# Selecting the first pair's slots ahead of its product and the other slots behind it

## The chip, the cores and the metric

The kernel runs on one core of one Trainium2 chip. The metric is the device time in microseconds (us) of one execution; it is run several times and the median counts.

A core has five engines that follow their own instruction lists and wait for each other by semaphores: TensorE (PE, matrix products, with a separate stream of weight loads), VectorE (DVE), ScalarE (ACT), GpSimd (POOL) and SyncE (SP), whose list here is mostly transfers. Sixteen DMA engines carry the transfers.

## The reference

Two layers run one after the other: the first mixes tokens by a short convolution, the second by sparse attention, and each is followed by a hierarchical mixture of experts (MoE) and a layer norm. All 1024 tokens have 1024 features. The MoE is what matters here:

```python
g_top = jnp.argmax(g_logits, axis=-1)                 # one of 8 groups for each token
e_val, e_loc = lax.top_k(e_logits, TOPK_IN_GROUP)     # two of the 8 experts in it
gate = jax.nn.softmax(e_val, axis=-1) * g_gate
...
def expert_block(args):
    xb, e = args
    h = jax.nn.silu(xb @ w1[e]) * (xb @ w3[e])        # w1, w3: 1024 x 256
    return h @ w2[e]                                  # w2: 256 x 1024
...
out = jnp.zeros_like(xt).at[row_tok].add(ys * row_w[:, None].astype(ys.dtype))
```

There are 64 experts in each layer, and every one is computed. Inputs and outputs are 32 bit floats.

## The kernel before

The memory on the chip is cut into 26 equal slots of one megabyte (128 partitions x 2048 floats). `take` hands out the slot that has been free longest, `give` returns one; what is written into a slot waits for the last readers of what was there. The order of the instructions on each engine is the order in which the program is written.

`moe(l, ...)` (L794) computes one MoE. An expert has 64 places for tokens, two experts make a pair (32 pairs, `NP`), four pairs make a group (8 groups, `GP` = 4), so a group has 512 places. `gather` (L823) brings the rows of a group's 128 tokens from memory on POOL's queue; block `NG`, gathered second, holds tokens of any group that are over 128. `parts` (L832) makes 0/1 matrices `sel` on DVE and splits the gathered rows into a high and a low part, in two halves for the first group: ACT writes the high part (L210), DVE the low (L211).

`select` (L849) turns them into `gt`, the tokens of the group's 512 places, feature by place: for each of 8 tiles `k` of 128 features four products (two blocks x high and low) of 128 x 512 add up in one PSUM buffer `rg` (three of them), and DVE or ACT by turns copies it to `gt[k]`. For the first group `select` runs before all pairs, and for every other group in the last pair of the group ahead of it, between `turn` and `down`.

A pair is: `up` (L863), the product of its 128 places with w1 and w3 into `ph`; `act` (L877), Silu on ACT and a multiplication on DVE; `turn` (L881), two transposes on PE; `down` (L888), the product with w2, scaled by ACT and DVE into the slot `yslot` and, for an overflow, `bslot`; `add` (L915) adds the pair before to the sums of the group.

The weights are 192 matrices of one megabyte per MoE. `prefetch(l, keep)` (L783) starts loads, in the order in which the pairs need them, as long as more than `keep` slots are free; they go to SP's queue if no other is named. `up` and `down` give their slots back after each half. The stage starts with two gathers, then `prefetch(l, 3, eng=nc.gpsimd)`, `parts(0)`, four products that only warm PE (L89), `select()`, and `yslot, bslot = self.take(), self.take()`.

Of the kernel before, what the change touches and what calls it, by code (L numbers as in the profile page):

```python
# [23 lines left out]
F32 = mybir.dt.float32  # L24
# [4 lines left out]
AF = mybir.ActivationFunctionType  # L29
# [4 lines left out]
P = 128  # L34
T = 1024
D = 1024
# [30 lines left out]
class Net:  # L67
# [726 lines left out]
    def moe(self, l, out, last=None, split=None):  # L794
# [3 lines left out]
        nc, S, W = self.nc, self.slots, self.W  # L798
        R_ = lambda v: v.bitcast(F32R)
        mm = nc.tensor.matmul  # L800
        ctx = ExitStack()
        psh = ctx.enter_context(self.tc.tile_pool(name="ps_h", bufs=1, space=PSUM))
        psr = ctx.enter_context(self.tc.tile_pool(name="ps_r", bufs=3, space=PSUM))
        psc = ctx.enter_context(self.tc.tile_pool(name="ps_c", bufs=1, space=PSUM))
        xr = {}
        gts = [self.take() for _ in range(2)]
        ms, hs = self.take(), self.take()
        sel = [S[ms][:, b * 512:(b + 1) * 512] for b in range(2)]
        hg, hT, io = (S[hs][:, a:b] for a, b in ((1024, 1280), (1280, 1536), (1536, 2048)))
        pick = [S[ms][:, 1024 + i * 256:1024 + (i + 1) * 256] for i in range(4)]  # L810
        gt = [S[gts[k // 4]][:, (k % 4) * 512:(k % 4 + 1) * 512] for k in range(KT)]
        nc.gpsimd.iota(io, pattern=[[1, 512]], base=0, channel_multiplier=0,
                       allow_small_or_imprecise_dtypes=True)
        xs, sums, scat, kept = {}, {}, [], []
# [8 lines left out]
        def gather(b):  # L823

            if b == 1:
                xr[0] = self.take()
            idx = (self.rows0 if b in (0, 1, 2, NG) else self.rows)[:, b:b + 1]
            nc.gpsimd.indirect_dma_start(
                out=xrow(b), out_offset=None, in_=self.xn[:, :],
                in_offset=bass.IndirectOffsetOnAxis(ap=idx, axis=0), bounds_check=T - 1, oob_is_err=False)  # L830

        def parts(g):  # L832


            for i in range(2):
                o, c = sel[i], g + i * NG
                nc.vector.tensor_scalar(R_(o), io, self.codes[:, 0, c:c + 1], None, op0=OP.is_equal)
                nc.vector.scalar_tensor_tensor(R_(o), io, self.codes[:, 1, c:c + 1], o, op0=OP.is_equal, op1=OP.add)
            v = []
            for i, b in ((0, g), (1, NG))[:1 if g else 2]:  # L840
                s = xs[i] = self.take()
                v.append([xrow(b).rearrange("s (q k) -> s k q", k=KT),
                          *(S[s][:, j * D:(j + 1) * D].rearrange("s (k q) -> s k q", k=KT) for j in range(2))])
            w = KT if g else KT // 2
            for k in range(0, KT, w):
                for a in v:
                    self.split(*(b[:, k:k + w] for b in a))

        def select():  # L849

            for k in range(KT):
                pt = psr.tile([P, 512], F32, name="rg")
                for i in range(2):
                    for j in range(2):
                        mm(pt, R_(S[xs[i]][:, j * D + k * P:j * D + (k + 1) * P]), R_(sel[i]),  # L855
                           start=i == 0 and j == 0, stop=i == 1 and j == 1)
                if k % 2:
                    nc.scalar.activation(gt[k], pt, AF.Copy)
                else:
                    nc.vector.tensor_copy(gt[k], pt)  # L860
            self.give(xs[0])

        def up(p):  # L863
            o = p % GP * P
            ph = psh.tile([P, 512], F32, name="ph")
            for m in range(2):
                for k in range(KT):
                    for q in range(2):
                        w = S[W[2 * p + q, m]]
                        mm(ph[q * CAP:(q + 1) * CAP, m * 256:(m + 1) * 256],  # L870
                           gt[k][:, o + q * CAP:o + (q + 1) * CAP], w[:, k * 256:(k + 1) * 256],
                           start=k == 0 and m == 0, stop=k == KT - 1, skip_group_check=True)
                self.give(*[W.pop((2 * p + q, m)) for q in range(2)])
                self.prefetch(l, 1 if p < 3 else 0)
            return ph

        def act(p, ph):  # L877
            nc.scalar.activation(hg, ph[:, :256], AF.Silu)  # L878
            nc.vector.tensor_mul(hg, hg, ph[:, 256:])  # L879

        def turn(p):  # L881
            px = psr.tile([P, 512], F32, name="rg")
            hv = hg.rearrange("s (q c) -> s c q", c=2)
            for c in range(2):
                nc.tensor.transpose(px[:, c * P:(c + 1) * P], hv[:, c], self.ident)
            nc.scalar.activation(hT, px[:, :256], AF.Copy)  # L886
# [20 lines left out]
        def places(p):  # L907

            o = pick[p % GP]
            nc.vector.tensor_scalar(R_(o[:, :P]), io[:, :P], self.srank[:, p:p + 1], None, op0=OP.is_equal)  # L910
            if p >= NP - GP:
                nc.vector.tensor_scalar(R_(o[:, P:]), io[:, P:2 * P], self.sr7[:, p % GP:p % GP + 1], None,
                                        op0=OP.is_equal)

        def add(p, h):  # L915

            i = p % GP
            for b in range(2 if p >= NP - GP else 1):
                if i == 0:
                    sums[b, h] = psc.tile([P, 512], F32, name=f"pc{b}{h}")  # L920
                for j in range(2):
                    mm(sums[b, h], R_(pick[i][:, b * P:(b + 1) * P]),
                       R_(S[yslot][:, j * D + h * 512:j * D + (h + 1) * 512]),
                       start=i == 0 and j == 0, stop=i == GP - 1 and j == 1 and b == 0)
# [4 lines left out]
        def beyond(p):  # L929

            nc.gpsimd.indirect_dma_start(  # L931
                out=self.Yov[l][:, :], out_offset=bass.IndirectOffsetOnAxis(ap=self.ovi[:, p:p + 1], axis=0),
                in_=share(p), in_offset=None, bounds_check=2 * P - 1, oob_is_err=False)

        def load_beyond():
            for j in range(2):
                nc.sync.dma_start(S[bslot][:, j * D:(j + 1) * D], self.Yov[l][j * P:(j + 1) * P])

        def residual(b, h):
            v = xrow(b)[:, h * 512:(h + 1) * 512]  # L940
            nc.vector.scalar_tensor_tensor(v, v, ALPHA, sums[0, h], op0=OP.mult, op1=OP.add)
# [12 lines left out]
        def finish(b):  # L954

            st = ln_st()
            for h in range(2):
                self.ln_stats(xrow(b), st, h)
            self.ln_done(xrow(b), st)
            scatter(b)  # L960
# [4 lines left out]
        def scale_rows():  # L965
            kept.append(NG)
            a = [S[xs[1]][:, j * D:(j + 1) * D].rearrange("s (k q) -> s k q", k=KT) for j in range(2)]
            nc.vector.tensor_add(xrow(NG).rearrange("s (q k) -> s k q", k=KT), *a)
            nc.vector.tensor_scalar(xrow(NG - 1), xrow(NG - 1), ALPHA, None, op0=OP.mult)
# [6 lines left out]
        def residual_sums(k, stop=False):  # L976
            b, i = ends[k]
            for h in range(2):
                mm(sums[i, h], self.ident, xrow(b)[:, h * 512:(h + 1) * 512], start=False, stop=stop)
# [15 lines left out]

        for b in (0, NG):
            gather(b)
        self.prefetch(l, 3, eng=nc.gpsimd)
        parts(0)
        self.warm(psr, "rg", io, WARM[1])  # L1000
        select()
        yslot, bslot = self.take(), self.take()
        self.prefetch(l, 0)
        for p in range(NP):
            g, i = divmod(p, GP)
            if p == NP - 1:
                residual_sums(0)
            ph = up(p)
            act(p, ph)
            places(p)  # L1010
            if p:
                add(p - 1, 0)
            turn(p)
            if p:
                add(p - 1, 1)
            if p == NP - 2:
                scale_rows()
            if i == GP - 1 and g + 1 < NG:
                select()
            down(p)  # L1020
            if g < NG - 1:
                beyond(p)
            if g and i == 0:
                for h in range(2):
                    residual(g - 1, h)
                finish(g - 1)
            if p < 2:
                gather(p + 1)
            if 0 < g < NG - 2 and i == 2:
                gather(g + 2)  # L1030
            if p == 2:
                self.load_ln(self.i["ln2_g"][l], self.i["ln2_b"][l], nc.scalar)
            if p == GP + 2:
                self.count_over()
            if i == GP - 2 and g + 1 < NG:
                parts(g + 1)
            if last and p == NP - 1:
                last()
            self.prefetch(l, 0)
            if p == NP - 2:  # L1040
                load_beyond()
# [958 lines left out]
```

## Time and profile before

| | before |
|---|---|
| median of 3 runs | 2250.32 us (2249.17 to 2250.35) |
| the profiled execution | 2252.98 us |
| its span in the profile | 2251.2 us |
| PE busy | 2116.3 us, 94% |
| DVE, ACT, POOL busy | 52%, 38%, 18% |
| first MoE, second MoE (selecting products to last sums) | 414 to 905 us, 1750 to 2238 us |

Every time in the profile is counted from the start of the span. Busy time of PE contains products that overlap with the next one, so a run of products is best read by the starts of its first and last. "PEclk" is the clock that the throttle granted to PE, 1.00 for 2.4 GHz and 0.50 for 1.2 GHz. A wait names what ended last.

### The profile page before, as it was taken

How to read it: one execution, taken by the hardware profiler on the slowest of the kernel's cores; microseconds unless marked ns; L12 is line 12 of the kernel's file. 1: busy time of each engine (PE TensorE's matmuls, PEld its weight loads, DVE VectorE, ACT ScalarE, POOL GpSimd, SP SyncE). 2: the span in 40 equal slices, each digit the busy share in tenths (PEclk: the TensorE clock that was granted, in tenths of full speed). 3: DMA queues.
4: the chain of work that ended last, by engine and by line, in shares of the span. 5: the costliest groups of instructions: out<-in, count | busy, mean ns of one | idle time of the engine just before them, and what ended most of it. 6: DMA issues, size and time to landing. Idle time of an engine off the chain costs nothing. (4 is left out here: it accounts for less than half of the span.)

```text
span 2251.2 us, 32795 instructions
## 1 busy us (share of the span) xinstructions
PE 2116.3 (94%) x12541; PEld 1547.7 (69%) x12541; DVE 1164.0 (52%) x2760; ACT 846.3 (38%) x1714; POOL 394.9 (18%) x477
## 2 busy tenths in 40 slices
PE   8999999799999999699998999999997998999997
PEld 7888888455555555677886899998886555555553
DVE  4333478432333333567878877774488233333333
ACT  3111211232333331356895877763211332333321
POOL 0000011110111110522332544322012111111101
PEclk9999999899999999899998999999999999999998
DMA  5113275599999999212211000003335799999995
GB/s 160 50 55 114 98 271 189 214 419 420 418 419 419 420 418 397 101 38 66 56 29 75 1 1 20 1 19 118 118 128 205 291 418 420 419 418 419 420 419 247
DMA packets 136777, 502.63 MB, mean 223 GB/s; under 512 B 23339, under 2 KB 69651, under 8 KB 86948
## 3 DMA queue, kind: packets, MB, share of 16 engines
q1 hardware_dynamic: 116608, 461.86, 52.1%
q0 software_dynamic: 16128, 32.09, 3.8%
q10 hardware_dynamic: 3876, 6.51, 0.8%
q8 instruction: 100, 1.64, 0.3%
q14 instruction: 65, 0.53, 0.1%
HBM read 476.70 MB, written 51.40 MB: 235 GB/s over the span
## 5 line engine op out<-in xcount | busy, mean ns | idle before, releaser
L870 PE MATMUL ph<-slot,slot 128*64 128x256 f32 x4096 | 461.5, 382 | 13.0 <-DVE nx L771 8.6
L870 PEld LDWEIGHTS ph<-slot,slot 128*64 128x64 f32 x4096 | 297.5, 138 | 193.1 <-issue 48.9
L901 DVE SCALAR_TENSOR_TENSOR slot<-rg,sgate,slot 128x512 fp32r<-128x512 f32 x128 | 96.1, 751 | 300.7 <-ACT slot L900 299.7
L896 PE MATMUL rg<-slot,slot 128*64 128x512 f32 x1024 | 233.8, 598 | 4.1 <-ACT slot L886 1.3
L210 ACT ACTIVATE slot<-slot 128x1024 fp32r<-128x1024 f32 (+2 forms) x151 | 119.0, 839 | 246.8 <-DVE slot L372 148.1
L222 PE MATMUL ps<-slot,slot 128*128 128x512 f32 x512 | 203.0, 396 | 0.8 <-DVE slot L211 0.8
L224 PE MATMUL ps<-slot,slot 128*128 128x512 f32 x512 | 199.6, 390 | 0.0
L223 PE MATMUL ps<-slot,slot 128*128 128x512 f32 x512 | 199.6, 390 | 0.0
L222 PE MATMUL po<-slot,slot 128*128 128x256 f32 (+1 forms) x544 | 189.9, 349 | 0.4 <-DVE slot L1699 0.4
L931 POOL DMA_INDIRECT Yov<-slot,ovi x56 | 55.5, 991 | 727.5 <-ACT slot L903 727.5
L223 PE MATMUL po<-slot,slot 128*128 128x256 f32 (+1 forms) x544 | 181.5, 334 | 0.0
L224 PE MATMUL po<-slot,slot 128*128 128x256 f32 (+1 forms) x544 | 181.5, 334 | 0.0
L211 DVE TENSOR_TENSOR slot<-slot,slot 128x1024 fp32r<-128x1024 f32 (+2 forms) x146 | 125.3, 895 | 89.9 <-ACT slot L210 88.8
L896 PEld LDWEIGHTS rg<-slot,slot 128*64 128x64 f32 x1024 | 67.8, 136 | 139.5 <-issue 114.6
L879 DVE TENSOR_TENSOR slot<-slot,ph 128x256 f32<-128x256 f32 x64 | 26.9, 420 | 232.9 <-ACT slot L878 232.9
L222 PE MATMUL pa<-slot,slot 128*128 128x512 f32 (+1 forms) x384 | 144.4, 376 | 0.2 <-DVE slot L211 0.2
L224 PE MATMUL pa<-slot,slot 128*128 128x512 f32 (+1 forms) x384 | 143.2, 373 | 0.0
L223 PE MATMUL pa<-slot,slot 128*128 128x512 f32 (+1 forms) x384 | 143.2, 373 | 0.0
L900 ACT ACTIVATE slot<-rg,sgate 128x512 fp32r<-128x512 f32 x128 | 87.6, 684 | 133.5 <-PE rg L896 133.5
L211 DVE TENSOR_TENSOR slot<-pT,slot 128x512 fp32r<-128x512 f32 (+1 forms) x160 | 101.6, 635 | 70.0 <-ACT slot L210 68.7
L855 PE MATMUL rg<-slot,slot 128*128 128x512 f32 x512 | 126.0, 403 | 6.2 <-ACT slot L210 4.1
L878 ACT ACTIVATE slot<-ph 128x256 f32<-128x256 f32 x64 | 24.6, 385 | 282.7 <-PE ph L870 282.7
(319 smaller groups left out, 3880.2 us busy)
## 6 DMA issues: line engine op xcount, KB each, us to landing
slot<-in_exp_w_dram SPq DMA_DIRECT2D x380, 1024.0 KB, 19.4
slot<-in_conv_w_in_dram SPq DMA_DIRECT2D x24, 512.0 KB, 3.8
slot<-in_attn_w_in_dram SPq DMA_DIRECT2D x17, 512.0 KB, 3.9
slot<-in_x_dram SPq DMA_DIRECT2D x16, 512.0 KB, 4.5
slot<-xres SPq DMA_DIRECT2D x16, 512.0 KB, 4.0
slot<-in_attn_w_out_dram SPq DMA_DIRECT2D x8, 1024.0 KB, 5.7
xn<-slot POOLq DMA_DIRECT2D x14, 512.0 KB, 3.0
slot<-in_conv_w_out_dram SPq DMA_DIRECT2D x8, 512.0 KB, 3.8
```

The lines of the kernel that those rows point to most:

```text
L210: self.nc.scalar.activation(hi.bitcast(F32R), raw, AF.Copy)
L211: (eng or self.nc.vector).tensor_sub(lo.bitcast(F32R), raw, hi)
L222: mm(out, ah.bitcast(F32R), bh.bitcast(F32R), start=start, stop=False)
L223: mm(out, ah.bitcast(F32R), bl.bitcast(F32R), start=False, stop=False)
L224: mm(out, al.bitcast(F32R), bh.bitcast(F32R), start=False, stop=stop)
L855: mm(pt, R_(S[xs[i]][:, j * D + k * P:j * D + (k + 1) * P]), R_(sel[i]), start=i == 0 and j == 0, stop=i == 1 and j == 1)
L870: mm(ph[q * CAP:(q + 1) * CAP, m * 256:(m + 1) * 256], gt[k][:, o + q * CAP:o + (q + 1) * CAP], w[:, k * 256:(k + 1) * 256], start=k == 0 ...
L879: nc.vector.tensor_mul(hg, hg, ph[:, 256:])
L896: mm(py[q * CAP:(q + 1) * CAP], hT[:, c * P + q * CAP:c * P + (q + 1) * CAP], w[:, c * D + n * 512:c * D + (n + 1) * 512], start=c == 0, s ...
L900: nc.scalar.activation(R_(hi), py, AF.Copy, scale=g)
L901: nc.vector.scalar_tensor_tensor(R_(lo), py, g, hi, op0=OP.mult, op1=OP.subtract)
L931: nc.gpsimd.indirect_dma_start(out=self.Yov[l][:, :], out_offset=bass.IndirectOffsetOnAxis(ap=self.ovi[:, p:p + 1], axis=0), in_=share(p), ...
```

## The change

The first group's selection is cut into two. `select_first` takes only the 128 places of the first pair, ahead of its product: 8 tiles x 4 products of 128 columns, gathered four tiles to a PSUM buffer, so that DVE makes one copy (of four pieces of 128) and ACT one. The other 384 places of the first group are selected by `select(P)` after `up(0)` and before `act(0)`. Later groups run `select()` as before, with the same products and copies.

The two slots of the outputs, `yslot` and `bslot`, are taken after `up(0)`, when the first weights have been released, and no longer ahead of the pairs. The first call of `prefetch` keeps two slots instead of three; the one with keep 0 behind `select` is gone; within pair 0 `up` keeps two instead of one.

```diff
@@ -846,19 +846,40 @@
                 for a in v:
                     self.split(*(b[:, k:k + w] for b in a))
 
-        def select():
+        def selected(pt, k, c, out):
+
+            for i in range(2):
+                for j in range(2):
+                    mm(pt, R_(S[xs[i]][:, j * D + k * P:j * D + (k + 1) * P]), R_(sel[i])[:, c],
+                       start=i == 0 and j == 0, stop=i == 1 and j == 1)
+            if out % 2:
+                nc.scalar.activation(gt[k][:, c], pt, AF.Copy)
+            else:
+                nc.vector.tensor_copy(gt[k][:, c], pt)
+
+        def select(lo=0):
 
             for k in range(KT):
                 pt = psr.tile([P, 512], F32, name="rg")
-                for i in range(2):
-                    for j in range(2):
-                        mm(pt, R_(S[xs[i]][:, j * D + k * P:j * D + (k + 1) * P]), R_(sel[i]),
-                           start=i == 0 and j == 0, stop=i == 1 and j == 1)
-                if k % 2:
-                    nc.scalar.activation(gt[k], pt, AF.Copy)
+                selected(pt[:, :512 - lo], k, slice(lo, 512), k)
+            self.give(xs[0])
+
+        def select_first():
+
+            for q in range(2):
+                pt = psr.tile([P, 512], F32, name="rg")
+                for k in range(4):
+                    for i in range(2):
+                        for j in range(2):
+                            f = j * D + (4 * q + k) * P
+                            mm(pt[:, k * P:(k + 1) * P], R_(S[xs[i]][:, f:f + P]), R_(sel[i])[:, :P],
+                               start=i == 0 and j == 0, stop=i == 1 and j == 1)
+                o = S[gts[q]].rearrange("p (k s) -> p k s", k=4)[:, :, :P]
+                v = pt.rearrange("p (k s) -> p k s", k=4)
+                if q:
+                    nc.scalar.activation(o, v, AF.Copy)
                 else:
-                    nc.vector.tensor_copy(gt[k], pt)
-            self.give(xs[0])
+                    nc.vector.tensor_copy(o, v)
 
         def up(p):
             o = p % GP * P
@@ -871,7 +892,7 @@
                            gt[k][:, o + q * CAP:o + (q + 1) * CAP], w[:, k * 256:(k + 1) * 256],
                            start=k == 0 and m == 0, stop=k == KT - 1, skip_group_check=True)
                 self.give(*[W.pop((2 * p + q, m)) for q in range(2)])
-                self.prefetch(l, 1 if p < 3 else 0)
+                self.prefetch(l, (2, 1, 1)[p] if p < 3 else 0)
             return ph
 
         def act(p, ph):
@@ -995,17 +1016,18 @@
 
         for b in (0, NG):
             gather(b)
-        self.prefetch(l, 3, eng=nc.gpsimd)
+        self.prefetch(l, 2, eng=nc.gpsimd)
         parts(0)
         self.warm(psr, "rg", io, WARM[1])
-        select()
-        yslot, bslot = self.take(), self.take()
-        self.prefetch(l, 0)
+        select_first()
         for p in range(NP):
             g, i = divmod(p, GP)
             if p == NP - 1:
                 residual_sums(0)
             ph = up(p)
+            if p == 0:
+                select(P)
+                yslot, bslot = self.take(), self.take()
             act(p, ph)
             places(p)
             if p:
```

PE, at the start of the first MoE (slots 3047 and 3064 or 3066 hold `sel` and the parts, 3045 and 3046 `gt`; L855 is the selecting product, L870 `up`, L885 `turn`, L896 `down`). Before:

```order
L89 MATMUL rg<-slot_3048,ident 128x512 x2
L855 MATMUL rg<-slot_3047,slot_3064 128x512 x2
L855 MATMUL rg<-slot_3047,slot_3065 128x512 x2
...
L855 MATMUL rg<-slot_3047,slot_3065 128x512 x2
L870 MATMUL ph<-slot_1922,slot_3045 64x256
L870 MATMUL ph<-slot_1924,slot_3045 64x256
...
L870 MATMUL ph<-slot_1928,slot_3046 64x256
L885 MATMUL rg<-ident,slot_3048 128x128 x2
L896 MATMUL rg<-slot_1930,slot_3048 64x512
L896 MATMUL rg<-slot_2055,slot_3048 64x512
```

Changed (L875 and L853 are the two selections, L891 `up`, L906 `turn`, L917 `down`):

```order
L89 MATMUL rg<-slot_3048,ident 128x512 x2
L875 MATMUL rg<-slot_3047,slot_3066 128x128 x2
L875 MATMUL rg<-slot_3047,slot_3067 128x128 x2
...
L875 MATMUL rg<-slot_3047,slot_3067 128x128 x2
L891 MATMUL ph<-slot_1922,slot_3045 64x256
L891 MATMUL ph<-slot_1924,slot_3045 64x256
...
L891 MATMUL ph<-slot_1928,slot_3046 64x256
L853 MATMUL rg<-slot_3047,slot_3066 128x384 x2
L853 MATMUL rg<-slot_3047,slot_3067 128x384 x2
...
L853 MATMUL rg<-slot_3047,slot_3067 128x384 x2
L906 MATMUL rg<-ident,slot_3048 128x128 x2
L917 MATMUL rg<-slot_1930,slot_3048 64x512
```

Ahead of pair 0's product stand the same 32 products, a quarter as wide; 32 more, of 384 columns, stand between it and its transposes.

ACT, from the last split on (L858 copies `gt`, L878 is `act`, L886 `turn`, L900 and L903 are `down`). Before:

```order
L210 ACTIVATE slot_3064<-slot_3048 128x512
L210 ACTIVATE slot_3065<-slot_3046 128x512
L858 ACTIVATE slot_3045<-rg 128x512 x2
L858 ACTIVATE slot_3046<-rg 128x512 x2
L878 ACT_TABLE_LOAD
L878 ACTIVATE slot_3048<-ph 128x256
L886 ACTIVATE slot_3048<-rg 128x256
L900 ACTIVATE slot_3125<-rg,sgate 128x512
```

Changed (L880 and L856 copy `gt`, L899 is `act`, L907 `turn`, L921 and L924 `down`):

```order
L210 ACTIVATE slot_3066<-slot_3048 128x512
L210 ACTIVATE slot_3067<-slot_3046 128x512
L880 ACTIVATE slot_3046<-rg 128x4x128
L856 ACTIVATE slot_3045<-rg 128x384 x2
L856 ACTIVATE slot_3046<-rg 128x384 x2
L899 ACT_TABLE_LOAD
L899 ACTIVATE slot_3048<-ph 128x256
L907 ACTIVATE slot_3048<-rg 128x256
```

The four copies of the second selection, and so the load of the activation table and the Silu, stand behind products that come after pair 0's.

POOL, at the same place (L828 gathers, L792 loads weights, L931 scatters what overflows). Before:

```order
L812 IOTA slot_3048 128x512
L828 DMA slot_3048<-xn,rows_92 128x1024
L828 DMA slot_3046<-xn,rows_92 128x1024
L792 DMA slot_3056<-in_exp_w_dram 128x2048
L792 DMA slot_3058<-in_exp_w_dram 128x2048
L931 DMA Yov_112<-slot_3126,ovi 256x1024
L828 DMA slot_3192<-xn,rows_92 128x1024
```

Changed (L952 scatters):

```order
L812 IOTA slot_3048 128x512
L828 DMA slot_3048<-xn,rows_92 128x1024
L828 DMA slot_3046<-xn,rows_92 128x1024
L792 DMA slot_3056<-in_exp_w_dram 128x2048
L792 DMA slot_3058<-in_exp_w_dram 128x2048
L792 DMA slot_3060<-in_exp_w_dram 128x2048
L952 DMA Yov_112<-slot_3201,ovi 256x1024
L828 DMA slot_3228<-xn,rows_92 128x1024
```

There is one load of weights more behind the two gathers, and on SP's queue one less.

## Rows read from the trace of the kernel before

**Rows 1.** Waits of PE, 427 to 900 us: who, for whom, total, times, longest.

```profile
PE rg L885 <- DVE slot L879: 12.2, 29, 1.0
...
PE ph L870 <- DMA slot<-in_exp_w_dram: 2.0, 2, 1.3
```

**Rows 2.** Windows: length, busy time by engine, PEclk, transfer share, GB/s.

```profile
440.00:450.00 10.00, 9.63 (x76) 5.63 (x74) 1.57 (x4) 2.72 (x5) 2.10 (x2) 1.00 0.88 328
450.00:475.00 25.00, 24.33 (x174) 13.50 (x171) 8.57 (x13) 8.92 (x13) 3.09 (x3) 1.00 1.02 418
```

**Rows 3.** Timeline of PE: start, duration, instruction, shape, count, idle before.

```profile
418.68 9.06 PE L855 MATMUL rg<-slot,slot 128*128 128x512 f32 x29 [0.32 <-DVE slot L211]
427.67 7.13 PE L870 MATMUL ph<-slot,slot 128*64 128x256 f32 x64
435.76 0.51 PE L885 MATMUL rg<-ident,slot 128*128 128x128 f32 x2 [0.96 <-DVE slot L879]
...
440.23 7.08 PE L870 MATMUL ph<-slot,slot 128*64 128x256 f32 x64
```

**Rows 4.** Windows, same columns, in the selecting products of the first MoE.

```profile
418.70:423.20 4.50, 4.50 (x11) 3.57 (x12) 2.88 (x4) 1.48 (x2) 0.00 (x0) 0.50 0.22 91
423.60:427.60 4.00, 4.00 (x19) 3.08 (x17) 1.40 (x3) 1.20 (x2) 0.00 (x0) 1.00 0.01 2
```

**Rows 5.** Timeline of ACT at the start of the first MoE.

```profile
416.39 3.19 ACT L210 ACTIVATE slot<-slot 128x512 fp32r<-128x512 f32 x3 [2.64 <-DMA slot<-xn,rows]
...
427.78 0.60 ACT L858 ACTIVATE slot<-rg 128x512 f32<-128x512 f32 x1 [1.21 <-PE rg L855]
428.39 1.28 ACT L878 ACT_TABLE_LOAD   x1
434.87 0.38 ACT L878 ACTIVATE slot<-ph 128x256 f32<-128x256 f32 x1 [5.19 <-PE ph L870]
```

**Rows 6.** Timeline of DVE at the start of the first MoE.

```profile
417.55 3.17 DVE L211 TENSOR_TENSOR slot<-slot,slot 128x512 fp32r<-128x512 f32 x3 [2.50 <-ACT slot L210]
...
435.29 0.42 DVE L879 TENSOR_TENSOR slot<-slot,ph 128x256 f32<-128x256 f32 x1 [7.72 <-ACT slot L878]
```

**Rows 7.** Timeline of POOL and of SP's queue at the start of the first MoE.

```profile
409.67 1.00 POOL L828 DMA_INDIRECT slot<-xn,rows  x1 [0.31 <-issue]
410.68 1.15 POOL L792 DMA_DIRECT2D slot<-in_exp_w_dram  x2
...
431.37 22.42 SPq L792 DMA_DIRECT2D slot<-in_exp_w_dram  x11
```

**Rows 8.** Timeline of PE in the attention stage, products of 128 and 384 columns.

```profile
1211.11 0.22 PE L222 MATMUL pL<-slot,slot 128*128 128x128 f32 x1
...
1212.29 0.28 PE L224 MATMUL pL<-slot,slot 128*128 128x128 f32 x1
...
1236.40 0.42 PE L223 MATMUL pL<-slot,slot 128*128 128x128 f32 x1
...
1237.26 0.41 PE L224 MATMUL pL<-slot,slot 128*128 128x128 f32 x1
...
1267.27 0.34 PE L223 MATMUL pL<-slot,slot 128*128 128x384 f32 x1
...
1267.98 0.34 PE L224 MATMUL pL<-slot,slot 128*128 128x384 f32 x1
```

**Rows 9.** Window of the attention stage, columns as in rows 2.

```profile
1231.50:1241.70 10.20, 10.19 (x48) 9.92 (x48) 4.34 (x26) 7.33 (x31) 2.74 (x4) 0.50 0.01 2
```

**Rows 10.** Timeline of PE behind two gaps, and the same four products without one.

```profile
527.77 9.51 PE L870 MATMUL ph<-slot,slot 128*64 128x256 f32 x64 [4.36 <-DVE nx L771]
...
882.22 1.98 PE L979 MATMUL pc<-slot,ident 128*128 128x512 f32 x4
...
901.62 3.50 PE L979 MATMUL pc<-slot,ident 128*128 128x512 f32 x4 [1.84 <-DVE slot L974]
```

**Rows 11.** Timeline of PE, second MoE.

```profile
1753.34 9.05 PE L855 MATMUL rg<-slot,slot 128*128 128x512 f32 x29 [0.32 <-DVE slot L211]
```

## The prediction

> **What bounds the kernel now.** I read the waits of TensorE (PE) in one MoE stage first, then the transfer share, then the start of the stage engine by engine, and last the rows elsewhere that price the new shapes. In 473 us of the first MoE PE waits 12.2 us for VectorE before its small transposes and 2.0 us for weights [rows 1]; nearly all the rest is work. The transfers are as full: 1.02 of the sixteen engines at 418 GB/s [rows 2]. So the two run side by side, PE is the bound, and the weights arrive just in time. What is added to PE after the start is added to the end, unless it fits into the 2.0 us.
>
> At the start, the last 29 of the 32 selecting products run without a gap from 418.68 to 427.67, the product of pair 0 follows with 7.13 us, and its transposes come at 435.76 after a gap of 0.96 [rows 3]. The clock is at the lower level (1.2 GHz, 0.50) until about 423.4, then at the upper one (2.4 GHz) [rows 4]. PE had to wait until 418.68 for halves of the gathered rows: ScalarE's (ACT's) last three begin at 416.39, when the second gather has landed, and VectorE's (DVE's) last three end at 417.55 + 3.17 = 420.72 [rows 5, 6]. Weights start again at 431.37, when the first half of pair 0's product releases its slots [rows 7].
>
> **The change part by part**, per MoE; there are two, and the second shows the same figure (its 29 products take 9.05 us) [rows 11].
>
> *First selection.* It has the same 32 products, 128 columns wide instead of 512. The narrow width doesn't cost a quarter: at the lower clock four steps of such products take 1237.26 - 1236.40 = 0.86, 0.215 each, and at the upper one eleven steps take 1.18, 0.107 each [rows 8]. The 29 that stand after 418.68 need 29 x 0.215 = 6.2 us at the lower clock, so the product of pair 0 starts at 424.9, **2.8 us earlier**. If the clock rises at 423.4 as now: 22 by then, 7 x 0.107 after, start at 424.2, 3.5 earlier. I take 2.8, since in the attention stage PE stood 10.2 us without a gap (10.19 busy) at 0.50 while mainly such narrow products ran [rows 9]. The splits are done at 420.72 and hold up neither half. The copies out of PSUM are two instead of eight: DVE's falls behind the second half's products and ACT's has 16 instructions of the product ahead of the first that reads it.
>
> The Trainium skill ("TensorE: Matmul & The Clock Gate", section "Back-to-back issue gap") speaks for the change: it puts an isolated stream of products at their columns over the clock, some 107 ns for 128 columns at 1.2 GHz, half of what rows 8 show. By it the first selection would end about 2.8 us sooner still, and the sum below would be 5.7 instead of 8.5 per MoE; the trace's products, each with its own weights to load, don't agree with it.
>
> *Third early load.* GpSimd (POOL) issues three loads instead of two at 410.68, one behind the gathers [rows 7]. It takes the place of one that starts when pair 0's product ends, so the same five are issued by the end of pair 0. Nothing else stands on POOL's queue there. It can hold back the gather, issued at 409.67 and waited for until 416.39 [rows 5, 7]: by nothing, as it is issued last of all, or by as much as its own transfer takes, one megabyte at 418 GB/s, 2.5 us [rows 2]. I take **+0.4**, near the lower end, since two loads already stand between it and the gather.
>
> *Product of pair 0.* The 64 products are the same, 7.13. If the clock is still low they pay: 0 to 2.4 us, since the product after the 4.36 us wait took 9.51 while the clock came back [rows 10] against 7.13. Rows 9 end about where 256-column products begin, so I take a rise some 2 us into it: **+1.0**.
>
> *Second selection.* 32 products of 384 columns, all of it new work: four steps take 1267.98 - 1267.27 = 0.71, 0.178 each [rows 8], 32 x 0.178 = **+5.7**. PE's columns in total stay equal (128 + 384), but 64 products cost more than 32 wide ones. Its copies alternate between two engines and three buffers, well inside the 0.71 of a tile.
>
> *The wait before the first transposes.* Act(0) now stands behind the second selection's copies on ACT. After the last product: 0.11 to the copy (427.67 to 427.78), a copy of 384, about 0.49 (between 0.38 for 256 and 0.60 for 512 columns), the table load 1.28, then 0.89 from the Silu's start (434.87) to the transposes (435.76) [rows 3, 5], by way of DVE's multiplication at 435.29 [rows 6]. That is 2.8 against 1.0 now, where the table load lay under the product: **+1.8**. Queued behind it are PE's transposes, down(0) and all later pairs, and DVE's places(0).
>
> *The clock after that wait.* A gap of 1.84 us was followed by products that took 3.50 us where the same four took 1.98, one of 4.36 us by 9.51 instead of 7.13 [rows 10]; gaps of 0.96 were not. 2.8 lies between. The price is 0 to 2.4; I take **+2.4**, as the work that follows is long.
>
> *Weights.* The next two loads start after down(0), at 440.2 now, and would start as much later as PE is late; by then as many are loaded as now. Between 440 and 450 the transfers are at 0.88 and only after that full [rows 2], so the whole stream moves by the same amount, and PE's late waits for weights stay.
>
> Sum per MoE: -2.8 + 0.4 + 1.0 + 5.7 + 1.8 + 2.4 = **+8.5**; two give +17.0. Against the profiled execution's 2252.98 that is 2270.0; it lay 2.7 above the median of the three runs, 2250.3, and to that the forecast is **2267.3**.
>
> **The rivals.**
> 1. *The clock is kinder.* Without the fall after the wait, 6.1 per MoE, 2262.5; if it also rises at 423.4 as now, -3.5 + 0.4 + 5.7 + 1.8 = 4.4, 2259.1. For it: the clock's changes hang on where the gaps fall. Against: rows 9 and 10.
> 2. *Longer low clock*: 2.4 instead of 1.0 on pair 0's product and 1.1 instead of 0.4 for the gather: 10.6 each, 2271.5.
> 3. *Narrow products at a quarter.* Eleven wide ones ran in 4.50 us at the lower clock [rows 4], 0.41; a quarter is 0.10. Then the last 13 products from 420.72 decide, a start at 422.0, and 5.6 is left of the 8.5: 2261.5. Rows 8 speak against it. The rule that is quoted above from the Trainium skill's page would lead here.
> 4. *Late weights swallow it (no change).* If PE waits at the end for weights that didn't move, 2.0 of at least 3.9 vanish in each stage: +1.9 each, 2254.1. Against: the loads behind down(0) move too.
> 5. *Faster: the weights decide.* One megabyte at 418 GB/s is 2.5 us [rows 2], and it is carried while the engines are idle. If the stage ends with its last weights and PE's additions lie inside waits for them, each stage ends 2.5 sooner: 2245.3. It decides from the point where PE's waits for weights exceed what PE gains in work, about 8 us; the trace has 2.0.
>
> **How the numbers follow.** Forecast (7 to 9.5 per MoE) 0.55, rival 1 0.22, rival 2 0.07, rival 3 0.03, rival 4 0.08, rival 5 0.05. About 0.2%, 4.5 us, is what a measurement of this kernel can tell from no change: faster 0.05, same 0.08, slower 0.87. The range 2257 to 2272 takes in the forecast, rivals 1 and 3 but for their smallest sums, and half of rival 2, some 0.82.
>
> **What the changed profile would show.** Right: 128-column products some 0.21 apart while the clock is low; pair 0's product beginning near 425; a run of 32 products of 384 columns behind it, of 5.7 us; a gap of 2.5 to 3 us before the first transposes, with the table load and the Silu inside; the clock low for some microseconds behind it; the next weights after down(0) some 8 us later, and unchanged steps of pairs from there on. Wrong: products of 128 columns 0.11 apart from the start on; a gap of about 1 us, or none; pairs that come faster than now; waits for weights that vanish late in the stage.

## The result, and the profile after

| | before | changed |
|---|---|---|
| median, same chip, four runs each | 2249.95 us (2249.17 to 2250.35) | 2266.57 us (2265.97 to 2269.87) |
| ratio to before | | 1.0075 (95% interval 1.0063 to 1.0087) |
| the profiled execution | 2252.98 us | 2265.97 us |
| its span in the profile | 2251.2 us | 2264.2 us |

The change costs 16.6 us; the forecast was 17.0, at 2267.3. The two spans differ by only 13.0, because the profiled execution of before lies 3.0 above its median and that of the changed kernel 0.6 below.

The waits of PE in the first MoE, 427 to 915 us (who, for whom, total, times, longest):

```profile
PE rg L906 <- DVE slot L900: 14.0, 29, 2.7
PE ph L891 <- DVE nx L771: 4.4, 1, 4.4
PE ph L891 <- DMA slot<-in_exp_w_dram: 2.5, 3, 1.3
```

Beside [rows 1], the wait for DVE before the transposes has grown from 12.2 to 14.0, and its longest is now 2.7. The waits for weights did not shrink: 2.5 instead of 2.0.

The timeline of PE at the start of the first MoE (start, duration, instruction, shape, count, idle before):

```profile
417.73 6.45 PE L875 MATMUL rg<-slot,slot 128*128 128x128 f32 x29 [0.64 <-DVE slot L211]
424.11 8.34 PE L891 MATMUL ph<-slot,slot 128*64 128x256 f32 x64
432.38 5.82 PE L853 MATMUL rg<-slot,slot 128*128 128x384 f32 x32
440.92 0.70 PE L906 MATMUL rg<-ident,slot 128*128 128x128 f32 x2 [2.72 <-DVE slot L900]
442.09 6.11 PE L917 MATMUL rg<-slot,slot 128*64 128x512 f32 x16 [0.47 <-ACT slot L907]
448.04 7.07 PE L891 MATMUL ph<-slot,slot 128*64 128x256 f32 x64
```

Read it against [rows 3], from start to start: the first selection takes 424.11 - 417.73 = 6.38 instead of 8.99. Pair 0's product takes 8.34 instead of 7.13, the second selection is new, the gap before the transposes is 2.72 instead of 0.96, and from the transposes to pair 1's product it is 7.12 instead of 4.47. Pair 1's product begins at 448.04; it was at 440.23.

What the gap is made of stands on ACT:

```profile
415.44 3.19 ACT L210 ACTIVATE slot<-slot 128x512 fp32r<-128x512 f32 x3 [1.48 <-DMA slot<-xn,rows]
...
438.24 0.49 ACT L856 ACTIVATE slot<-rg 128x384 f32<-128x384 f32 x1 [0.90 <-PE rg L853]
438.73 1.28 ACT L899 ACT_TABLE_LOAD   x1
440.03 0.38 ACT L899 ACTIVATE slot<-ph 128x256 f32<-128x256 f32 x1
```

The last copy of the second selection, the table load and the Silu follow each other without a gap, and the Silu's input had been ready since 432.4. In [rows 5] the same table load lay under the product. The first of these rows also shows the second gather in use at 415.44, 0.95 earlier than in [rows 5].

The clock, in windows (length, busy time and count of PE, PEld, DVE, ACT and POOL, PEclk, transfer share, GB/s):

```profile
425.00:426.00 1.00, 1.00 (x8) 0.60 (x6) 0.00 (x0) 0.00 (x0) 0.00 (x0) 0.50 0.00 0
427.00:428.00 1.00, 1.00 (x14) 0.62 (x12) 0.00 (x0) 0.00 (x0) 0.00 (x0) 1.00 0.00 0
437.00:438.00 1.00, 1.00 (x7) 0.88 (x6) 0.46 (x1) 0.34 (x1) 0.00 (x0) 1.00 0.00 0
...
444.00:445.00 1.00, 1.00 (x6) 0.33 (x4) 0.00 (x0) 0.00 (x0) 0.00 (x0) 0.50 0.00 0
448.00:449.00 1.00, 1.00 (x12) 0.65 (x10) 0.00 (x0) 0.70 (x2) 0.00 (x0) 1.00 0.00 0
```

It is still at the lower level almost two microseconds into pair 0's product, at the upper one through the second selection, down again through down(0) behind the gap of 2.72, and up when pair 1 begins. The second MoE repeats it:

```profile
1758.46 6.45 PE L875 MATMUL rg<-slot,slot 128*128 128x128 f32 x29 [0.64 <-DVE slot L211]
1764.84 8.69 PE L891 MATMUL ph<-slot,slot 128*64 128x256 f32 x64
1773.46 5.84 PE L853 MATMUL rg<-slot,slot 128*128 128x384 f32 x32
1782.02 0.70 PE L906 MATMUL rg<-ident,slot 128*128 128x128 f32 x2 [2.72 <-DVE slot L900]
1783.19 6.28 PE L917 MATMUL rg<-slot,slot 128*64 128x512 f32 x16 [0.47 <-ACT slot L907]
1789.31 7.07 PE L891 MATMUL ph<-slot,slot 128*64 128x256 f32 x64
```

### The profile page after: what moved, and what is told of

It is laid out like the page before. It is cut to its first block, busy times and chain, and to the rows that moved or that the text cites. A ratio compares the mean times of both kernels' runs of the same rounds, so it can differ in the third digit from the quotient of the medians.

```text
span 2264.2 us, 32929 instructions
## 1 busy us (share of the span) xinstructions
PE 2125.4 (94%) x12605; PEld 1557.6 (69%) x12605; DVE 1163.8 (51%) x2762; ACT 846.1 (37%) x1716; POOL 394.8 (17%) x479
## 5 line engine op out<-in xcount | busy, mean ns | idle before, releaser
L891 PE MATMUL ph<-slot,slot 128*64 128x256 f32 x4096 | 463.6, 383 | 13.6 <-DVE nx L771 8.6
L891 PEld LDWEIGHTS ph<-slot,slot 128*64 128x64 f32 x4096 | 299.1, 138 | 193.7 <-issue 47.2
L917 PE MATMUL rg<-slot,slot 128*64 128x512 f32 x1024 | 238.9, 609 | 3.8 <-ACT slot L907 0.9
L952 POOL DMA_INDIRECT Yov<-slot,ovi x56 | 55.5, 990 | 744.5 <-ACT slot L924 726.3
L917 PEld LDWEIGHTS rg<-slot,slot 128*64 128x64 f32 x1024 | 69.0, 139 | 143.5 <-issue 120.0
L900 DVE TENSOR_TENSOR slot<-slot,ph 128x256 f32<-128x256 f32 x64 | 26.9, 420 | 222.8 <-ACT slot L899 222.8
L921 ACT ACTIVATE slot<-rg,sgate 128x512 fp32r<-128x512 f32 x128 | 87.5, 684 | 137.7 <-PE rg L917 137.7
L899 ACT ACTIVATE slot<-ph 128x256 f32<-128x256 f32 x64 | 24.6, 384 | 273.0 <-PE ph L891 273.0
L853 PE MATMUL rg<-slot,slot 128*128 128x512 f32 (+1 forms) x512 | 116.0, 384 | 0.0
```

What stands on the lines that cost most here:

```text
L891: mm(ph[q * CAP:(q + 1) * CAP, m * 256:(m + 1) * 256], gt[k][:, o + q * CAP:o + (q + 1) * CAP], w[:, k * 256:(k + 1) * 256], start=k == 0 ...
L917: mm(py[q * CAP:(q + 1) * CAP], hT[:, c * P + q * CAP:c * P + (q + 1) * CAP], w[:, c * D + n * 512:c * D + (n + 1) * 512], start=c == 0, s ...
L921: nc.scalar.activation(R_(hi), py, AF.Copy, scale=g)
L952: nc.gpsimd.indirect_dma_start(out=self.Yov[l][:, :], out_offset=bass.IndirectOffsetOnAxis(ap=self.ovi[:, p:p + 1], axis=0), in_=share(p), ...
```

## The experiments

The theory under test is the forecast's: PE is the bound at the start of the stage, and the cost is the second selection, the gap behind it and the lower clock. The rival is that the place of the slots and the weights decide. Two measures tell them apart, both taken from PE's timeline. The **start** is the time from the small product of L722 (it ends the routing) to pair 1's product. The **late stretch** is the time from pair 26's product to pair 28's, where PE waits for weights; without waits it takes 32.28 (pairs 18 to 20 of before, 691.32 to 723.60). All in us, with first and second MoE divided by a slash; the last column is the number of weight loads that are issued in the first MoE ahead of down(0)'s releases:

| kernel | median | ratio to before | start | late stretch | loads |
|---|---|---|---|---|---|
| before | 2249.8 to 2249.95 | 1 | 30.73 / 30.68 | 35.81 / 34.49 | 5 |
| changed | 2266.57 | 1.0075 | 38.52 / 41.09 | 36.20 / 35.94 | 5 |
| selection only | 2268.96 | 1.0083 | 39.40 / 41.42 | 36.60 / 35.74 | 5 |
| slots only | 2245.58 | 0.9980 | 31.65 / 30.45 | 33.50 / 32.60 | 6 |
| act first | 2258.09 | 1.0039 | 34.89 / 35.81 | 36.25 / 36.09 | 5 |
| busy gap | 2263.23 | 1.0057 | 37.18 / 38.53 | 36.20 / 36.02 | 5 |
| two pairs | 2250.87 | 1.0007 | 29.60 / 30.79 | 36.31 / 36.10 | 5 |
| output first | 2250.2 | 1.0002 | 30.19 / 30.55 | 35.64 / 34.40 | 5 |

Single executions of one kernel lie up to 8 us apart (two pairs: 2246.85 to 2254.66; before: 2247.09 to 2253.14 over all its runs), so medians carry the verdicts and the traces only the places.

**Selection only.** The changed kernel with the loads and the slots as near to before as the cut selection allows: two early loads instead of three, yslot ahead of the pairs, bslot behind the second selection.

```diff
-                self.prefetch(l, (2, 1, 1)[p] if p < 3 else 0)
+                self.prefetch(l, 1 if p < 3 else 0)
...
-        self.prefetch(l, 2, eng=nc.gpsimd)
+        self.prefetch(l, 3, eng=nc.gpsimd)
...
         select_first()
+        yslot = self.take()
...
-                yslot, bslot = self.take(), self.take()
+                bslot = self.take()
```

> The selection in two parts alone; the loads and the slots of the outputs as before (two early loads on POOL, one slot of the outputs taken ahead of the pairs, the other behind the second selection). If PE's own order is the cause, all of the loss is here: 2264 to 2269 us, pair 1's product some 8 us later than before in each MoE. If the third early load had paid back part of it by letting the weights run ahead, this kernel is about 5 us slower than the changed one, 2271 us.

2268.96 (2266.48 to 2271.65), ratio 1.0083 [1.0066, 1.0100]. The whole loss is there without the third early load. The ratio lies within the interval of the changed kernel, so beside the cut selection the early load and the later slots neither cost nor bring anything that these runs can tell from noise. Its timeline shows the longer price of the low clock on pair 0's product, and the same gap:

```profile
424.94 9.67 PE L891 MATMUL ph<-slot,slot 128*64 128x256 f32 x64
434.54 5.82 PE L853 MATMUL rg<-slot,slot 128*128 128x384 f32 x32
443.08 0.50 PE L906 MATMUL rg<-ident,slot 128*128 128x128 f32 x2 [2.72 <-DVE slot L900]
```

**Slots only.** The kernel before with its single selection; three early loads, two slots kept in pair 0, both output slots taken behind `up(0)`.

```diff
-                self.prefetch(l, 1 if p < 3 else 0)
+                self.prefetch(l, (2, 1, 1)[p] if p < 3 else 0)
...
-        self.prefetch(l, 3, eng=nc.gpsimd)
+        self.prefetch(l, 2, eng=nc.gpsimd)
...
         select()
-        yslot, bslot = self.take(), self.take()
-        self.prefetch(l, 0)
...
             ph = up(p)
+            if p == 0:
+                yslot, bslot = self.take(), self.take()
```

> The other half alone: one selection of 512 columns as before, but three early loads, two slots kept within pair 0, and the slots of the outputs taken after pair 0's product. If PE is the bound, nothing is gained: 2248.5 to 2251.5 us, with a shift of up to 1 us per MoE where the third load stands beside the gather. If the weights decide, one megabyte ahead is worth 2.5 us per MoE: 2245 us.

2245.58 (2244.73 to 2248.33), ratio 0.9980 [0.9970, 0.9989]: faster than before by 4.3 us, only 0.2% but with an interval clear of 1, where my theory had nothing. The start has hardly changed (31.65 and 30.45); the late stretch is shorter by 2.31 and 1.89, together 4.2, about what the medians gain. (The start and the pairs between give 1.2 of it back in these two traces, one execution each.) Pairs 26 to 28 of before, then of this kernel; the window ends at 845, in the middle of pair 28's product:

```profile
807.10 7.85 PE L870 MATMUL ph<-slot,slot 128*64 128x256 f32 x64
...
821.68 3.67 PE L870 MATMUL ph<-slot,slot 128*64 128x256 f32 x32 [0.68 <-DMA slot<-in_exp_w_dram]
826.65 3.67 PE L870 MATMUL ph<-slot,slot 128*64 128x256 f32 x30 [1.30 <-DMA slot<-in_exp_w_dram]
842.91 2.33 PE L870 MATMUL ph<-slot,slot 128*64 128x256 f32 x20
```

```profile
810.67 7.08 PE L870 MATMUL ph<-slot,slot 128*64 128x256 f32 x64
823.24 4.05 PE L870 MATMUL ph<-slot,slot 128*64 128x256 f32 x34
827.91 3.67 PE L870 MATMUL ph<-slot,slot 128*64 128x256 f32 x30 [0.62 <-DMA slot<-in_exp_w_dram]
844.17 1.03 PE L870 MATMUL ph<-slot,slot 128*64 128x256 f32 x8
```

Of three waits one is left: pair 26's product takes 7.08 instead of 7.85 (that wait stands inside the run and has no bracket), the wait of 0.68 is gone, and that of 1.30 is 0.62. The first five microseconds of pair 0's product, before and then here, show where the weights got ahead:

```profile
427.67:432.67 5.00, 5.00 (x47) 3.36 (x48) 0.00 (x0) 1.88 (x2) 0.00 (x0) 1.00 0.12 18
```

```profile
430.88:435.88 5.00, 5.00 (x47) 3.35 (x48) 0.00 (x0) 1.88 (x2) 0.00 (x0) 1.00 0.82 234
```

The selection gives back one slot when it ends. Before, yslot takes a slot that is free already and bslot that one, and no load is left room until the product's first half releases its weights. Here a load goes into it at once, at 430.53: 234 GB/s instead of 18.

**Output first.** Is that load the cause, or the third one behind the gathers? Slots only, with yslot taken behind the selection, so that it gets the slot in the load's stead; the third early load stays.

```diff
         select()
+        yslot = self.take()
         for p in range(NP):
...
-                yslot, bslot = self.take(), self.take()
+                bslot = self.take()
```

> The kernel before with the three early loads and the later bslot of the slots-only kernel, but yslot taken right behind the selection, so that it and not a load gets the slot that the selection releases. Theory that the gain of the slots-only kernel (2245.6) comes from the load that starts at the selection's end, 4 us ahead of the first release by pair 0's product, and puts the whole stream of weights ahead: here 5 loads are issued ahead of down(0) as in the kernel before, the lead is gone, PE waits late for weights as before (3.5 and 2.2 us around pair 27), 2249 to 2251. Theory that the third load behind the gathers is what pays: 2245 to 2246.5. Theory that the gain was a kinder clock between the stages: either time, with PE's late waits for weights as short as in the slots-only kernel.

2250.2 (2246.81 to 2251.82), ratio 1.0002 [0.9993, 1.0011]: the gain is gone, the late stretch is back at 35.64 and 34.40, and the transfers of the same five microseconds are at 21 GB/s:

```profile
426.90:431.90 5.00, 5.00 (x47) 3.36 (x48) 0.00 (x0) 1.88 (x2) 0.00 (x0) 1.00 0.16 21
```

So the third load alone brings nothing: one load fewer follows it within pair 0. What pays is a sixth load ahead of down(0), and it needs the slot that the selection releases. That load without the third early one was not tried.

**Act first.** The changed kernel with act(0) ahead of the second selection.

```diff
             ph = up(p)
+            act(p, ph)
             if p == 0:
                 select(P)
                 yslot, bslot = self.take(), self.take()
-            act(p, ph)
```

> The changed kernel with act(0) written ahead of the second selection, so that the table load runs under pair 0's product and the Silu under the selecting products. If the wait of 2.7 us before the first transposes and the low clock behind it are two of the terms (2.7 + 2.5 per MoE), both vanish: 2255 to 2258 us, no gap before the first transposes and the clock at 1.00 from pair 0's product on. If the loss lies in the loads or only in the second selection's length, it stays above 2262 us.

2258.09 (2256.01 to 2260.26), ratio 1.0039 [1.0025, 1.0053], 8.5 below the changed kernel:

```profile
425.05 9.10 PE L891 MATMUL ph<-slot,slot 128*64 128x256 f32 x64
434.08 6.00 PE L853 MATMUL rg<-slot,slot 128*128 128x384 f32 x32
439.92 0.39 PE L906 MATMUL rg<-ident,slot 128*128 128x128 f32 x2
440.94 3.65 PE L917 MATMUL rg<-slot,slot 128*64 128x512 f32 x16 [0.63 <-ACT slot L907]
444.42 7.08 PE L891 MATMUL ph<-slot,slot 128*64 128x256 f32 x64
```

The transposes follow the selection without a gap, and down(0) is at the upper clock, 3.65 instead of 6.11. That is at the upper edge of what was expected (2255 to 2258), and the clock was not at 1.00 from pair 0's product on: that product takes 9.10 here. The forecast's two terms, 1.8 + 2.4 = 4.2 per MoE and 8.4 for both, come close to the 8.5, but what goes is not quite the same. In the first MoE of this trace the whole gap of 2.7 is saved, also the 0.96 that stood there before, and 2.6 of the fall; pair 0's product takes 0.8 more and the first selection begins 0.9 later than in the changed kernel, so that the start is 3.63 shorter (5.28 in the second MoE).

**Busy gap.** The changed kernel with three products behind the second selection that compute nothing needed and only fill the wait for act(0); the profile shows each as two records.

```diff
                 select(P)
+                self.warm(psr, "rg", io, 3)
```

> The changed kernel with three warming products (512 columns, into a buffer that nobody reads) behind the second selection, where PE waits 2.7 us for the Silu. They take about 2.6 us at the upper clock and put nothing on the path, so the gap stays filled and the clock should not fall: if the fall is a term of its own, down(0) takes 3.65 us again instead of 6.1 to 6.3, and the time is about 2.5 us per MoE less, 2260 to 2263 us. If the products are slow there for another reason, the time stays at 2266 us.

2263.23 (2261.03 to 2263.81), ratio 1.0057 [1.0040, 1.0074].

```profile
439.75 2.74 PE L89 MATMUL rg<-slot,ident 128*128 128x512 f32 x6
442.63 0.50 PE L906 MATMUL rg<-ident,slot 128*128 128x128 f32 x2
443.61 3.65 PE L917 MATMUL rg<-slot,slot 128*64 128x512 f32 x16 [0.47 <-ACT slot L907]
447.09 7.08 PE L891 MATMUL ph<-slot,slot 128*64 128x256 f32 x64
```

The transposes come as late behind the selection as in the changed kernel (442.63 - 434.07 = 8.56; there 8.54). From there to pair 1's product it is 4.46 instead of 7.12: the fall of the clock costs 2.66 in this MoE, and the gap itself makes it fall. In the second MoE it is 4.46 instead of 7.29, 2.83. By medians the gain over the changed kernel is 3.3, of the 5.5 that the two falls are worth; in the first MoE of this trace pair 0's product gave 1.2 of it back (9.56 against 8.34).

**Two pairs.** Act first, and the cut in the middle: the first selection over the 256 places of two pairs (two tiles to a buffer, four copies), the second over the other 256.

```diff
-            for q in range(2):
+            H = 2 * P
+            for q in range(4):
                 pt = psr.tile([P, 512], F32, name="rg")
-                for k in range(4):
+                for k in range(2):
...
-                            mm(pt[:, k * P:(k + 1) * P], R_(S[xs[i]][:, f:f + P]), R_(sel[i])[:, :P],
+                            mm(pt[:, k * H:(k + 1) * H], R_(S[xs[i]][:, f:f + P]), R_(sel[i])[:, :H],
...
             ph = up(p)
+            act(p, ph)
             if p == 0:
-                select(P)
+                select(2 * P)
                 yslot, bslot = self.take(), self.take()
-            act(p, ph)
```

> The changed kernel with act(0) ahead of the second selection, and the first selection over the 256 places of two pairs (two tiles to a PSUM buffer, four copies), the second over the other 256. Theory that a narrow product is bound by its weight load (0.21 us at 1.2 GHz whatever is under 256 columns): the first 29 products still take 6.2 us, the second 32 take 32 x 0.118 = 3.8 instead of 5.8 us, so 2.0 less per MoE than with act(0) first alone: 2258.1 - 4.0 = 2254. Theory that columns count: the first 29 take 29 x 0.107 x 2 x 2 / 2 = 6.2 at 1.2 GHz too, but would be longer than those of 128 columns by a third or more, the sum of both selections stays, 2258. Theory that a fuller PE raises the clock sooner: pair 0's product in 7.1 to 7.5 instead of 9 us, another 1.5 per MoE, 2251.

2250.87 (2246.85 to 2254.66), ratio 1.0007 [0.9998, 1.0016]. Two things are in its timeline:

```profile
417.69 5.01 PE L876 MATMUL rg<-slot,slot 128*128 128x256 f32 x29 [0.73 <-DVE slot L211]
422.63 7.13 PE L892 MATMUL ph<-slot,slot 128*64 128x256 f32 x64
429.69 4.61 PE L853 MATMUL rg<-slot,slot 128*128 128x256 f32 x32
434.13 0.41 PE L907 MATMUL rg<-ident,slot 128*128 128x128 f32 x2
```

```profile
419.00:420.00 1.00, 1.00 (x7) 1.00 (x7) 1.00 (x2) 0.00 (x0) 0.00 (x0) 0.50 1.05 442
420.00:421.00 1.00, 1.00 (x8) 1.00 (x8) 0.33 (x1) 0.17 (x1) 0.00 (x0) 0.70 0.93 393
421.00:422.00 1.00, 1.00 (x11) 1.00 (x10) 0.22 (x1) 0.42 (x1) 0.00 (x0) 1.00 0.58 246
```

First, the clock rises at about 420.6, three microseconds into the products of 256 columns, where in the changed kernel it stayed low through those of 128 columns and until about 426.6. At the lower level a step takes 0.213 us with 256 columns as with 128, and after the rise 0.12. So the wider products, twice the work, are *sooner* done (4.94 against 6.38, start to start), and pair 0's product runs at its 7.13; of the three expectations the third is nearest. Second, the start is as short as before or shorter (29.60 and 30.79), and still nothing is gained: the late stretch is 36.31 and 36.10, 0.5 and 1.6 longer than before. What PE gains at the start without a sixth load, it waits for weights in pairs 26 and 27. This trace is of the fastest of ten executions, 4.0 below their median, so it shows the places and not the median's sum. PE and the weights are both the bound, and only the slots-only kernel moves the weights; no run joins the two.

## Why the prediction was right

The time, the sign and the mechanism were right: 16.6 us were lost where 17.0 were forecast, in the wait, the clock and the second selection. That the two come within 0.4 us is partly luck: the terms add up to 18.2 in the traces, and other places give some back (below). Term by term, per MoE:

| term | forecast | first MoE | second MoE |
|---|---|---|---|
| first selection, 29 products | -2.8 | -2.6 | -2.6 |
| gather and splits | +0.4 | -1.0 | +1.1 |
| pair 0's product at the low clock | +1.0 | +1.2 | +1.6 |
| second selection | +5.7 | +5.8 | +5.8 |
| wait before the first transposes | +1.8 | +1.8 | +1.8 |
| clock after it (transposes, down(0)) | +2.4 | +2.6 | +2.8 |
| start of pair 1's product | +8.5 | +7.8 | +10.4 |

*The first selection.* Narrow products cost 6.38 / 29 = 0.22 each, as [rows 8] had them at 0.215, and rival 3 falls. The figure that the prediction takes from the Trainium skill ("TensorE: Matmul & The Clock Gate", section "Back-to-back issue gap"), given there for isolated products, would have made it 0.107 here. It doesn't hold for this trace's products, which each load their own weights: they take twice that.

*The gather* is the one term whose size was wrong in each stage. It was to be the third load's transfer that holds it back. From the second gather's issue to its use it is 5.75 us with three loads (409.69 to 415.44) and 6.72 with two (409.67 to 416.39), and over the other kernels 5.8 to 7.0 with three and 6.4 with two. So the load has no price there that a run shows; the term moves by about 1 either way. In the second MoE every kernel with the act or the selection moved has its products of the first selection begin about a microsecond later behind L722 than before (10.2 in the changed kernel, 9.1 before). POOL issues the gathers later there: in the traces of those five kernels its wait ends with DVE's L711, in the other three with L739 or L740, which come earlier. Why it waits for another instruction was not followed up.

*The wait and the clock* were right to 0.4. The busy gap confirms the clock alone; between it and act(0) first lie 5.1 us, about two whole gaps of 2.7. Rival 1 (a kinder clock) falls by down(0) at 0.50, rival 2 (a longer low clock) fits selection only, with 9.67 on pair 0's product, better than the changed kernel.

*Weights.* The step held for the changed kernel: five loads ahead of down(0) as before, the next two with its releases, and the late stretch stayed (36.20 against 35.81, and 35.94 against 34.49, even somewhat longer). Rival 4 falls by that. But the reason that I gave for rival 5 was too small: "the trace has 2.0" counts only the waits that show as gaps. Against 32.28 without waits, PE lost 3.5 and 2.2 us there, and a sixth early load brings 4.3 us in all, close to the 5.0 of that rival. The changed kernel misses it because its second selection still reads the slot that a single selection releases: the second part of the change, which pays by itself, is cancelled by the first. (This follows from the count of loads and from the late stretch; no run gave the changed kernel a sixth load.)

*Between and behind.* 7.8 + 10.4 are 18.2, yet the spans differ by 13.0. Along the first MoE 1.9 come back, along the second 1.2 and in the attention stage 1.9. Part of that hangs on the clock: four products that [rows 10] had at 3.50 behind a wait of 1.84 take 1.98 in the changed kernel, behind the same wait:

```profile
909.09 1.98 PE L1000 MATMUL pc<-slot,ident 128*128 128x512 f32 x4 [1.85 <-DVE slot L995]
```

The slots-only kernel has 1.98 there too, the output-first kernel 3.54, with no difference in that place of the program. At the end of the second MoE the same products take 3.07 before and 1.98 in the changed kernel. So this part is the spread of single executions; what made the attention stage shorter was not looked into.

## What to carry to other kernels

Before splitting a run of products to start the next stage sooner, price the narrow products by the trace and not by their columns, and see what stands on an in-order engine behind the moved copies: here an activation that had been hidden, with its table load, came to the path and took the clock with it. Where PE and the stream of weights are both full, a gain at either alone vanishes in the other; count the loads that are issued ahead of the first release, and take buffers for outputs only after loads have taken what is free. The kernel before with that one change of slots (2245.58, ratio 0.9980) is the best of this case.

## What the runs showed of the hardware

The clock did not come up equally soon behind products of different width. In all these stretches PE's records leave no gap, and the clock is at the lower level at their start. Counted from the start of the last 29 selecting products, it was up after 2.9 us in both MoE of two pairs (256 columns), and after 4.1 to 6.1 us in the six of before, slots only and output first (512 columns). In the eight of the other kernels it was not up within the 6.4 us of 128-column products, but 2.5 to 5.2 us into pair 0's product behind them. The spread at one and the same width is large, and the clock had not fallen at the same moment before these products, so what part the width has in it isn't shown.

At the lower level products of 128 and of 256 columns come at the same rate, 0.213 us from start to start (changed, two pairs), and those of 512 at 0.427 (before). At the upper one the 32 products of 256 columns in two pairs took 434.13 - 429.69 = 4.44, 0.139 each. But most of their steps are 0.12, as expected; five longer ones, at the first product and where the fourth and the sixth tile begin, add the rest. There are three buffers `rg`, so waiting for one is likely there; the profile names no wait.

A wait of 1.85 us was followed by a fall of the clock in some executions and not in others (3.50 and 1.98 for the same four products), one of 2.72 in all four cases that the traces of the changed kernel and of selection only show.
